# A transformer block on one core: the first MLP matrix by Strassen's scheme on 2x2 blocks

## Chip, core and metric

One core of a Trainium2 chip runs the whole block in one launch. The metric is the device time of a launch in microseconds (us). Engines are called PE or TensorE (matrix products), DVE or VectorE, ACT or ScalarE, POOL or GpSimd, and SP, which issues DMA transfers. PEld is the load of a matmul's stationary tile. Every engine works through its own list of instructions in order; an instruction waits for the results and the free buffers that it needs.

## What is computed

One layer on T = 1024 tokens of width D = 1024, in float32: RMS norm, a wide input projection, two kinds of attention (A: dilated windows; B: compressed, selected and windowed blocks, with gates), an output projection added to the residual, RMS norm, an MLP of width 4096 with squared ReLU, and a last RMS norm:

```
h_res = h_res + mixed @ w_out
h = rms_norm(h_res, norm_mlp)
h_res = h_res + square(relu(h @ w_up)) @ w_down
return rms_norm(h_res, norm_final)
```

## The kernel before

Each float32 product is made of three matmuls: a tile is split into hi (rounded) and lo (the rest), and hi x hi, hi x lo, lo x hi are summed in PSUM. `split` makes both: a copy on ACT, a subtraction on DVE (L94 and L95, or L97 and L98 with a scale); where the source is a product, POOL subtracts (L1035).

Up to about 690 us the kernel makes projections and attention. The list `ORD = [5, 7, 6, 4, 3, 2, 1, 0]` is the order of the eight 128-token tiles in attention B. The output projection is cut into pieces (`out_proj(i, half)`, half 0 for A's heads, half 1 for B's) that are pumped into the attention as its tiles get ready; a piece makes 12 matmuls for 512 columns into a bank F (L704 to L706), and DVE adds it to the residual rows `hr(i)` (tiles called `st`, L708). The last pieces, of tiles 1 and 0, follow the attention. Before each, POOL sums a tile's heads into `ob` (L842), PE transposes `ob`, ACT and DVE split it (`mh`, `ml`) and L704 begins.

In the MLP, tokens 512 to 1023 (`H0`) come first. `h2_step` transposes rows of `hr`, scales by the gain and splits into `h2h`, `h2l`; rows are not normalised there, the factor 1/(mean square + eps) is applied when down is added (L1061, `r2q`). w_up is cut into 32 feature tiles f of 128 columns. `up(f)` makes for each token half 8 x 3 matmuls of 512 columns (L1024 to L1026), and `up_act` the squared ReLU: ACT relu, DVE product (L1033), ACT copy `uh` (L1034), POOL `ul` (L1035). `down(f0, t, last)` takes two feature tiles, one 128-token tile and two column cuts: 6 matmuls each (L1058 to L1060), which DVE adds to `hr(t)` (L1061). The main loop makes up for the next two feature tiles while down uses the two of before; weights arrive as 512 KB blocks (`wur`, `wdr`) one or two tiles ahead, in buffers of their own. PSUM has four banks in turn for `up` and `dn`. No order is written out by hand here: the scheduler of the framework sets it from dependencies, priorities and buffers.

## Time and profile before

| | us |
|---|---|
| median of 3 runs | 1425.83 (1423.37 to 1430.28) |
| the profiled execution's own time | 1424.83 |
| span in its profile (first to last instruction) | 1423.0 |
| TensorE busy | 1350.6 |
| VectorE, ScalarE, GpSimd busy | 791.9, 621.3, 478.7 |

The span is one execution's. "Busy" sums the time in which an engine runs an instruction; a busy TensorE is not one at its peak. An idle engine that nobody waits for costs nothing. The granted clock is that of TensorE, 1.00 for the upper of its two levels.

### The profile page before, as it was taken

The page shows a single profiled execution, that of the slowest core. Times are in us where ns is not written, and L with a number is a line of the kernel's source. Part 1 is how long each engine was busy: PE and PEld are TensorE (multiplying, and loading weights), DVE is VectorE, ACT ScalarE, POOL GpSimd, SP SyncE. Part 2 cuts the span into 40 slices and gives each one's busy share as a digit, 9 for nine tenths or more (in the row PEclk, how much of TensorE's full clock was granted, in tenths as well). Part 3 has the DMA queues.
Part 4 walks back from the last instruction along what each step waited for, and adds up shares of the span by engine and source line. Part 5 has one row for each costly group of instructions (what it writes and reads, how often), then busy time and mean ns, then how long its engine had stood idle before and what let it go on. Part 6 is the DMA issues. An engine that isn't in the chain of part 4 may idle for free.

```text
span 1423.0 us, 23380 instructions
## 1 busy us (share of the span) xinstructions
PE 1350.6 (95%) x9083; PEld 1144.6 (80%) x9083; DVE 791.9 (56%) x1624; ACT 621.3 (44%) x1108; POOL 478.7 (34%) x704
## 2 busy tenths in 40 slices
...
PEclk9999999999999999999899999999999999999999
...
GB/s 187 67 123 123 89 166 63 208 186 129 88 152 180 167 146 132 149 130 107 118 104 45 30 47 58 60 45 30 56 49 60 45 30 59 45 60 45 1 0 118
DMA packets 285198, 131.64 MB, mean 93 GB/s; under 512 B 219040, under 2 KB 272288, under 8 KB 285088
## 3 DMA queue, kind: packets, MB, share of 16 engines
...
## 4 chain that ended last, share of the span: by engine, by line
PE 71%; DVE 8%; DMA 7%; issue 5%; POOL 4%; ACT 4%; SPq 1%; POOLq 0%; DVEq 0%; ACTq 0%
PE dn L1060 8%; PE dn L1058 8%; PE dn L1059 8%; PE up L1026 8%; PE up L1025 8%; PE up L1024 8%; PE F L334 3%; PE F L335 3%; PE F L336 3%; DMA pt<-hl 2%; PE T L359 2%; PE S L417 2%; PE S L419 1%; DVE ns L428 1%; ACT ns L433 1%
## 5 line engine op out<-in xcount | busy, mean ns | idle before, releaser
L1035 POOL TENSOR_TENSOR ul<-ua,uh 128x512 fp32r<-128x512 f32 x64 | 83.6, 1306 | 608.2 <-ACT uh L1034 608.2
L1061 DVE SCALAR_TENSOR_TENSOR st<-dn,r2q,st 128x512 f32<-128x512 f32 (+1 forms) x257 | 191.8, 747 | 157.6 <-PE dn L1060 157.6
L1060 PE MATMUL dn<-wdh,ul 128*128 128x512 f32 (+1 forms) x514 | 202.6, 394 | 0.0
L1058 PE MATMUL dn<-wdh,uh 128*128 128x512 f32 (+1 forms) x514 | 202.4, 394 | 0.0
L1059 PE MATMUL dn<-wdl,uh 128*128 128x512 f32 (+1 forms) x514 | 202.3, 394 | 0.0
L1024 PE MATMUL up<-h2h,wuh 128*128 128x512 f32 x480 | 187.1, 390 | 1.0 <-ACT wuh L94 1.0
L1026 PE MATMUL up<-h2h,wul 128*128 128x512 f32 x480 | 187.0, 390 | 0.5 <-DVE wul L95 0.5
L1025 PE MATMUL up<-h2l,wuh 128*128 128x512 f32 x480 | 187.0, 390 | 0.0
L334 PE MATMUL F<-wh,hh 128*128 128x256 f32 (+1 forms) x576 | 166.3, 290 | 6.7 <-DVE st L213 3.2
L335 PE MATMUL F<-wl,hh 128*128 128x256 f32 (+1 forms) x576 | 165.6, 288 | 2.4 <-DVE wl L95 2.4
L336 PE MATMUL F<-wh,hl 128*128 128x256 f32 (+1 forms) x576 | 164.6, 286 | 0.0
L1032 ACT ACTIVATE ua<-up 128x512 f32<-128x512 f32 x60 | 35.5, 591 | 230.9 <-PE up L1026 230.9
L433 ACT ACTIVATE ns<-ns,mn 128x640 f32<-128x640 f32 (+7 forms) x152 | 110.8, 748 | 35.1 <-POOL mn L432 20.8
L449 POOL TENSOR_TENSOR hl<-ns,hl 128x640 f16<-128x640 f32 (+5 forms) x67 | 105.6, 1577 | 33.2 <-ACT hl L447 26.9
L334 PEld LDWEIGHTS F<-wh,hh 128*128 128x128 f32 x576 | 109.6, 191 | 8.9 <-DVE st L213 3.6
L1059 PEld LDWEIGHTS dn<-wdl,uh 128*128 128x128 f32 x514 | 96.5, 188 | 23.1
L1060 PEld LDWEIGHTS dn<-wdh,ul 128*128 128x128 f32 x514 | 96.4, 188 | 23.1
L1058 PEld LDWEIGHTS dn<-wdh,uh 128*128 128x128 f32 x514 | 96.5, 188 | 22.5
L95 DVE TENSOR_TENSOR wul<-wur,wuh 128x1024 fp32r<-128x1024 f32 x32 | 39.5, 1234 | 134.7 <-ACT wuh L94 134.7
L335 PEld LDWEIGHTS F<-wl,hh 128*128 128x128 f32 x576 | 110.4, 192 | 3.8 <-DVE wl L95 3.2
L336 PEld LDWEIGHTS F<-wh,hl 128*128 128x128 f32 x576 | 110.1, 191 | 0.5
L1024 PEld LDWEIGHTS up<-h2h,wuh 128*128 128x128 f32 x480 | 90.1, 188 | 20.8 <-ACT wuh L94 1.4
...
## 6 DMA issues: line engine op xcount, KB each, us to landing
wur<-in_w_up_dram SPq DMA_DIRECT2D x32, 512.0 KB, 4.1
wdr<-in_w_down_dram SPq DMA_DIRECT2D x32, 512.0 KB, 4.2
wr<-in_w_in_dram SPq DMA_DIRECT2D x44, 256.0 KB, 2.9
st<-in_x_dram SPq DMA_DIRECT2D x8, 512.0 KB, 6.0
wor<-in_w_out_dram SPq DMA_DIRECT2D x16, 256.0 KB, 3.6
ns<-in_xT_dram SPq DMA_DIRECT2D x7, 512.0 KB, 5.4
out_dram<-st SPq DMA_DIRECT2D x7, 512.0 KB, 2.6
w<-in_w_k_dram SPq DMA_DIRECT2D x4, 512.0 KB, 5.5
```

Source lines behind the costliest of these rows:

```text
L334: pe.matmul(ps, hh[:, k, ts], hi, start=k == 0, stop=False)
L335: pe.matmul(ps, hh[:, k, ts], lo, start=False, stop=False)
L336: pe.matmul(ps, hl[:, k, ts], hi, start=False, stop=k == KD - 1)
L433: u["exp"] = act.activation(ns[:, :n * 128], ns[:, :n * 128], AF.Exp, scale=-1.0, bias=mn[:, j:j + 1])
L449: pool.tensor_sub(lo, p, hi)
L1024: pe.matmul(ps, hi[:, k], h2h[:, k, hs], start=k == 0, stop=False)
L1025: pe.matmul(ps, hi[:, k], h2l[:, k, hs], start=False, stop=False)
L1026: pe.matmul(ps, lo[:, k], h2h[:, k, hs], start=False, stop=k == KD - 1)
L1058: pe.matmul(ps, uh[:, ts], wh[:, cs], start=j == 0, stop=False)
L1059: pe.matmul(ps, uh[:, ts], wl[:, cs], start=False, stop=False)
L1060: pe.matmul(ps, ul[:, ts], wh[:, cs], start=False, stop=j == NB - 1)
L1061: dve.scalar_tensor_tensor(o[:, cs], ps, r2q[:, t:t + 1], o[:, cs], op0=OP.mult, op1=OP.add)
```

## The change

Both factors of the first MLP product are cut into 2x2 blocks: w_up for a pair g of feature tiles into four blocks of 512 x 128 (k halves and the two tiles), the tokens into halves H0 and H1. Seven block products of 4 x 3 matmuls replace eight; there are 16 rounds g. The stationary tiles are sums of w_up's blocks, made per round (`w_prep`: five named combinations, then `w_split` into `wa` to `we`); the moving ones are sums of token blocks B11, B21, B22, T1 to T4, made once (`h2_first` for H0, `h2_second` for H1, which needs both halves). Sums of products, in float32, are made on DVE out of PSUM (`up`), and `c_done` makes the squared ReLU, `uh` and `ul`. For the sums to hold, rows must be normalised before they are combined: `out_proj`'s half 1 now squares, takes a power (L722 in the changed kernel) and scales `hr(i)` in place.

Memory is laid out anew: tiles of 128 x 512 float32 (2 KB in a partition) share places by `tag`. `u2` and `u3` hold quarters of w_down as they land (`d_load`) and later `uh` and `ul` of the second feature tile for H1; `cA` and `cB` hold two w_up blocks and later `c12` and `c22`. All PSUM tiles of the MLP come from the banks T, O, F (two each or fewer) and S (three) of the attention stage; down uses S.

```diff
@@ -706,6 +711,17 @@
                 pe.matmul(ps, ml[:, k], wh[:, cs], start=False, stop=k == 3)
             o = hr(i)[:, cs]
             dve.scalar_tensor_tensor(o, ps, rmm[:, half, i:i + 1], o, op0=OP.mult, op1=OP.add)
+            if half == 0:
+                return
+            if c == 0:
+                st["q"] = wop.tile([128, T], BF, name="mhq", tag="mh", bufs=2)
+            act.activation(st["q"][:, cs], o, AF.Square, accum_out=ssq[:, i, c:c + 1])
+            if c == 1:
+                r = r2[:, i:i + 1]
+                dve.tensor_scalar(r, ssq[:, i, 0:1], ssq[:, i, 1:2], D * EPS, op0=OP.add, op1=OP.add)
+                pool.tensor_tensor(r, r, expo[:, :1], op=OP.pow)
+                for n in range(2):
+                    mv(n, hr(i)[:, n * 512:n * 512 + 512], hr(i)[:, n * 512:n * 512 + 512], i, r2)
 
         return [prep] + [lambda c=c: part(c) for c in range(T // WC)]
...
+    def w_prep(g, first=False):
+        if g >= NP:
+            return []
+        A11, A12, A21, A22 = (RW[g, b] for b in range(4))
+
+        def s1():
+            if not first:
+                w_split(g, 1, "a", A11)
+            w_split(g, 4, "d" if first else "b", A22)
+
+        def s2():
+            dve.tensor_sub(A11, A11, A21)
+            dve.tensor_add(A21, A21, A22)
+            dve.tensor_sub(A22, A22, A11)
+            w_split(g, 6, "c", A22)
+
+        def s3():
+            if not first:
+                w_split(g, 2, "d", A12)
+            dve.tensor_sub(A12, A12, A22)
+
+        def s4():
+            w_split(g, 7, "e", A11)
+
+        return [s1, s2, s3, s4]
...
+    def d_load(g, q):
+        j, c = q % 2, q // 2
+        t = RD[g, q] = small("u%d" % (2 + j))
+        sp.dma_start(t, A["w_down"][(2 * g + j) * 128:(2 * g + j + 1) * 128, c * 512:c * 512 + 512])
+
+    def d_split(g, q):
+        j, c = q % 2, q // 2
+        if c == 0:
+            WD[g, j] = ml[0].tile([128, 2, D], F32R, name="dn", bufs=2)
+        t = WD[g, j][:, :, c * 512:c * 512 + 512]
+        split(t[:, 0], t[:, 1], RD.pop((g, q)))
...
+    UT = {(0, 0): ("v0", "v1"), (1, 0): ("v2", "v3"), (0, 1): ("u0", "u1"), (1, 1): ("u2", "u3")}
+
+    def c_done(g, f, h, a):
+        hi, lo = U[g, f, h] = [small(x, F32R, "uh" if n == 0 else "ul") for n, x in enumerate(UT[f, h])]
+        dve.scalar_tensor_tensor(a, a, 0.0, a, op0=OP.max, op1=OP.mult)
+        act.activation(hi, a, AF.Copy)
+        pool.tensor_sub(lo, a, f32(hi))
+
+    def up(g):
+        y = {n: bank(x, [128, 512], 2) for n, x in ((1, "T"), (4, "O"), (6, "T"), (2, "F"), (7, "O"), (5, "S"), (3, "S"))}
+        for q in range(2):
+            d_load(g, q)
+        prod(g, 1, y[1])
+        c11 = small("u0", name="c11")
+        act.activation(c11, y[1], AF.Copy)
+        w_split(g, 5, "a", RW[g, 2])
+        for q in range(2):
+            d_split(g, q)
+        for q in range(2, 4):
+            d_load(g, q)
+        prod(g, 4, y[4])
+        prod(g, 6, y[6])
+        c12 = small("cA", name="c12")
+        dve.tensor_add(c12, y[6], c11)
+        w_split(g, 3, "b", RW[g, 1])
+        w_load(g + 1, 2, "r2")
+        w_load(g + 1, 1, "r3")
+        prod(g, 2, y[2])
+        dve.tensor_add(c11, y[2], c11)
+        c_done(g, 0, 0, c11)
+        prod(g, 7, y[7])
+        c22 = small("cB", name="c22")
+        dve.tensor_add(c22, y[7], c12)
+        c21 = small("u1", name="c21")
+        dve.scalar_tensor_tensor(c21, y[4], -1.0, c22, op0=OP.mult, op1=OP.add)
+        c_done(g, 1, 0, c21)
+        for q in range(2, 4):
+            d_split(g, q)
+        prod(g, 5, y[5])
+        dve.tensor_add(c22, y[5], c22)
+        dve.tensor_add(c12, y[5], c12)
+        c_done(g, 1, 1, c22)
+        prod(g, 3, y[3])
+        dve.tensor_add(c12, y[3], c12)
+        c_done(g, 0, 1, c12)
...
+            ps = bank("S", [128, 512])[:, :cs.stop - cs.start]
+            for j in range(2):
+                uh, ul = U[g, j, h]
+                wd = WD[g, j]
+                pe.matmul(ps, uh[:, ts], wd[:, 0, cs], start=j == 0, stop=False)
+                pe.matmul(ps, uh[:, ts], wd[:, 1, cs], start=False, stop=False)
+                pe.matmul(ps, ul[:, ts], wd[:, 0, cs], start=False, stop=j == 1)
+            dve.scalar_tensor_tensor(o[:, cs], ps, r2[:, t:t + 1], o[:, cs], op0=OP.mult, op1=OP.add)
...
+    def h2_second(j):
+        raw = ml[0].tile([128, 4, 512], F32, name="wdx", tag="dn", bufs=2)
+        T1, T2, T3, T4 = (raw[:, n] for n in range(4))
+        ps = h2_ps(H1, j)
+        g = gm32[:, j:j + 1]
+        act.activation(T3, ps, AF.Copy, scale=g)
+        dve.scalar_tensor_tensor(T1, ps, g, f32(XH["B11"][:, j]), op0=OP.mult, op1=OP.subtract)
+        dve.tensor_sub(T1, T1, f32(XL["B11"][:, j]))
+        ps = h2_ps(H1, j + 4)
+        g = gm32[:, j + 4:j + 5]
+        dve.scalar_tensor_tensor(T2, ps, g, T1, op0=OP.mult, op1=OP.subtract)
+        dve.scalar_tensor_tensor(T3, ps, g, T3, op0=OP.mult, op1=OP.subtract)
+        split(XH["B22"][:, j], XL["B22"][:, j], ps, scale=g)
+        pool.tensor_sub(T4, T2, f32(XH["B21"][:, j]))
+        dve.tensor_sub(T4, T4, f32(XL["B21"][:, j]))
+        for x, t, e in (("T2", T2, dve), ("T3", T3, pool), ("T4", T4, dve), ("T1", T1, pool)):
+            act.activation(XH[x][:, j], t, AF.Copy)
+            e.tensor_sub(XL[x][:, j], t, f32(XH[x][:, j]))
...
+    for g in range(NP):
+        last = g == NP - 1
+        if g:
+            up(g)
...
+            fin["j"] = ml[0].tile([128, D], F32, name="sqj", tag="we", bufs=1)
+        else:
+            w_load(g + 1, 0, "cA")
+            w_load(g + 1, 3, "cB")
+        jobs = [] if last else w_prep(g + 1)
+        for i, t in enumerate(TO):
+            down(g, t, last)
+            if i >= 2 and jobs:
+                jobs.pop(0)()
```

**Order on POOL at the end of the attention stage.** `ot`, `oc`, `ob` are the head sums of a tile, `rmm` the norm factor of half 1, `ul` the rest of an activation. Before:

```order
L842 TENSOR_TENSOR oc_9790<-ot0_9937,oc_9790 128x512
L840 TENSOR_TENSOR den_10327<-den_10327,gate_81 128x8
L841 TENSOR_TENSOR ot_10142<-ot_10142,den_10327 128x8x64
L842 TENSOR_TENSOR ob_10141<-ot_10142,oc_9790 128x512
L117 TENSOR_TENSOR rmm_560<-ssm_559,expo_59 128x1
L1035 TENSOR_TENSOR ul_10362<-ua_10487,uh_10361 128x512
```

Now, where `r2` is the power of a row's sum of squares (the first one is tile 1's, the second tile 0's):

```order
L857 TENSOR_TENSOR ot_10191<-ot_10191,den_10383 128x8x64
L722 TENSOR_TENSOR r2_563<-r2_563,expo_59 128x1
L858 TENSOR_TENSOR ob_10190<-ot_10191,oc_9827 128x512
L117 TENSOR_TENSOR rmm_567<-ssm_566,expo_59 128x1
L722 TENSOR_TENSOR r2_563<-r2_563,expo_59 128x1
L1073 TENSOR_TENSOR ul_10774<-c11_10594,uh_10773 128x512
L1171 TENSOR_TENSOR T1l_10415<-wdx_10601,T1h_10408 128x512
L1167 TENSOR_TENSOR wdx_10601<-wdx_10601,B21h_10406 128x512
L1171 TENSOR_TENSOR T3l_10417<-wdx_10601,T3h_10410 128x512
L1171 TENSOR_TENSOR T1l_10415<-wdx_10629,T1h_10408 128x512
```

Behind tile 1's last piece a power now stands between the two steps that make tile 0's `ob`, and twelve subtractions for T1, T4 and T3 follow, where only the `ul` rows stood.

**Order on DVE where the second token half is made.** Before, each step is one split out of a transposed bank T (`h2l`), then weight splits:

```order
L98 SCALAR_TENSOR_TENSOR h2l_10349<-T_10590,gvec_58,h2h_10348 128x512
L98 SCALAR_TENSOR_TENSOR h2l_10349<-T_10603,gvec_58,h2h_10348 128x512
L95 TENSOR_TENSOR wdl_10656<-wdr_10648,wdh_10655 128x1024
L95 TENSOR_TENSOR wdl_10665<-wdr_10648,wdh_10664 128x1024
L95 TENSOR_TENSOR wul_10661<-wur_10649,wuh_10660 128x1024
L1033 SCALAR_TENSOR_TENSOR ua_10628<-O_10522,ua_10628 128x512
L95 TENSOR_TENSOR wul_10670<-wur_10652,wuh_10669 128x1024
L1033 SCALAR_TENSOR_TENSOR ua_10633<-F_10523,ua_10633 128x512
```

Now, in one step j (`wdx` holds T1 to T4 in float32; B11l, B22l, T2l, T4l are lo parts):

```order
L1164 SCALAR_TENSOR_TENSOR wdx_10629<-T_10638,gm32_564,wdx_10629 128x512
L1165 SCALAR_TENSOR_TENSOR wdx_10629<-T_10638,gm32_564,wdx_10629 128x512
L1171 TENSOR_TENSOR T4l_10418<-wdx_10601,T4h_10411 128x512
L1171 TENSOR_TENSOR T2l_10416<-wdx_10629,T2h_10409 128x512
L98 SCALAR_TENSOR_TENSOR B22l_10414<-T_10638,gm32_564,B22h_10407 128x512
L1168 TENSOR_TENSOR wdx_10629<-wdx_10629,B21l_10413 128x512
L1160 SCALAR_TENSOR_TENSOR wdx_10672<-T_10673,gm32_564,B11h_10405 128x512
L1161 TENSOR_TENSOR wdx_10672<-wdx_10672,B11l_10412 128x512
L1171 TENSOR_TENSOR T4l_10418<-wdx_10629,T4h_10411 128x512
L1164 SCALAR_TENSOR_TENSOR wdx_10672<-T_10681,gm32_564,wdx_10672 128x512
L1165 SCALAR_TENSOR_TENSOR wdx_10672<-T_10681,gm32_564,wdx_10672 128x512
L1171 TENSOR_TENSOR T2l_10416<-wdx_10672,T2h_10409 128x512
```

Where one row per bank stood, some nine stand for two banks, half of them with both inputs in SBUF.

**Order on DVE and PE in a round of the MLP.** Before, on DVE (`ua` is the squared ReLU, `st` the residual, x7 means seven rows alike):

```order
L1033 SCALAR_TENSOR_TENSOR ua<-up,ua 128x512
L1061 SCALAR_TENSOR_TENSOR st<-dn,r2q,st 128x512 x7
L1033 SCALAR_TENSOR_TENSOR ua<-up,ua 128x512
L95 TENSOR_TENSOR wul<-wur,wuh 128x1024
L1061 SCALAR_TENSOR_TENSOR st<-dn,r2q,st 128x512
L1033 SCALAR_TENSOR_TENSOR ua<-up,ua 128x512
L1061 SCALAR_TENSOR_TENSOR st<-dn,r2q,st 128x512 x7
L95 TENSOR_TENSOR wdl<-wdr,wdh 128x1024 x2
```

Now (rows of one round; `dn` is a quarter of w_down, c11 to c22 the four blocks of the result):

```order
L95 TENSOR_TENSOR dn_13111<-u2_13090,dn_13111 128x512
L1101 SCALAR_TENSOR_TENSOR c21_13186<-O_13084,c22_13184 128x512
L95 TENSOR_TENSOR dn_13114<-u3_13092,dn_13114 128x512
L1071 SCALAR_TENSOR_TENSOR c21_13186<-c21_13186 128x512
L1106 TENSOR_TENSOR c22_13184<-S_13088,c22_13184 128x512
L1107 TENSOR_TENSOR c12_13145<-S_13088,c12_13145 128x512
L1071 SCALAR_TENSOR_TENSOR c22_13184<-c22_13184 128x512
L1110 TENSOR_TENSOR c12_13145<-S_13089,c12_13145 128x512
L95 TENSOR_TENSOR dn_13111<-u2_13117,dn_13111 128x512
L95 TENSOR_TENSOR dn_13114<-u3_13119,dn_13114 128x512
L1071 SCALAR_TENSOR_TENSOR c12_13145<-c12_13145 128x512
L1127 SCALAR_TENSOR_TENSOR st_5707<-S_13238,r2_563,st_5707 128x512
```

Between the last products and the first evacuation of down stand sums, squares and the splits of w_down; L1110 reads product 3's bank behind the square of `c22`.

On PE, before, down's chunks (`dn`) and up's matmuls alternate with weights split a round ahead:

```order
L1058 MATMUL dn_11611<-wdh_11441,uh_11379 128x512
L1059 MATMUL dn_11611<-wdl_11442,uh_11379 128x512
L1060 MATMUL dn_11611<-wdh_11441,ul_11380 128x512
L1024 MATMUL up_11655<-h2h_10348,wuh_11446 128x512
L1025 MATMUL up_11655<-h2l_10349,wuh_11446 128x512
L1026 MATMUL up_11655<-h2h_10348,wul_11447 128x512
L1024 MATMUL up_11655<-h2h_10348,wuh_11446 128x512
L1025 MATMUL up_11655<-h2l_10349,wuh_11446 128x512
```

Now (F is product 2 of the next round, S the chunks of down):

```order
L1064 MATMUL F_13388<-B21l_10413,wd_13330 128x512
L1065 MATMUL F_13388<-B21h_10406,wd_13330 128x512
L1063 MATMUL F_13388<-B21h_10406,wd_13330 128x512
L1064 MATMUL F_13388<-B21l_10413,wd_13330 128x512
L1124 MATMUL S_13238<-dn_13111,uh_13167 128x512
L1125 MATMUL S_13238<-dn_13111,uh_13167 128x512
L1065 MATMUL F_13388<-B21h_10406,wd_13330 128x512
L1126 MATMUL S_13238<-dn_13111,ul_13168 128x512
L1124 MATMUL S_13238<-dn_13114,uh_13188 128x512
L1125 MATMUL S_13238<-dn_13114,uh_13188 128x512
```

Six chunks of down follow there, all of tokens H0, and then product 4 of the next round with the weight tile `wb`, which is split out of `cB`.

## Rows read from the trace of the kernel before

**Rows 1.** The page: the span, TensorE's busy time with its share and instructions, and the clock granted in 40 equal slices (tenths).
```profile
span 1423.0 us, 23380 instructions
PE 1350.6 (95%) x9083; PEld 1144.6 (80%) x9083; DVE 791.9 (56%) x1624; ACT 621.3 (44%) x1108; POOL 478.7 (34%) x704
PEclk9999999999999999999899999999999999999999
```

**Rows 2.** Busy time of each engine (us, instructions) in two stretches; behind it the granted clock, the mean busy share of the DMA engines, GB/s.
```profile
600.00:620.00 20.00, 18.34 (x215) 14.83 (x213) 17.54 (x43) 16.72 (x32) 13.48 (x16) 1.00 0.85 156
760.00:1400.00 640.00, 640.00 (x2781) 521.77 (x2780) 276.73 (x356) 128.29 (x179) 77.40 (x62) 1.00 0.14 42
```

**Rows 3.** Waits from 760 to 1400 us: VectorE's for TensorE, total us, times, longest.
```profile
DVE st L1061 <- PE dn L1060: 154.0, 180, 2.5
```

**Rows 4.** Timeline of PE in the MLP: start, us of one, engine, line, operation, tiles.
```profile
1001.01 0.39 PE L1024 MATMUL up<-h2h,wuh 128*128 128x512 f32 x1
1003.73 0.39 PE L1024 MATMUL up<-h2h,wuh 128*128 128x512 f32 x1
...
1004.41 0.40 PE L1058 MATMUL dn<-wdh,uh 128*128 128x512 f32 x1
1009.77 0.39 PE L1060 MATMUL dn<-wdh,ul 128*128 128x512 f32 x1
```

**Rows 5.** Groups of instructions from 760 to 1400 us: shapes, count, busy us, mean ns; idle before and what ended it.
```profile
L1061 DVE SCALAR_TENSOR_TENSOR st<-dn,r2q,st 128x512 f32<-128x512 f32 x238 | 178.5, 750 | 154.1 <-PE dn L1060 154.0
L1035 POOL TENSOR_TENSOR ul<-ua,uh 128x512 fp32r<-128x512 f32 x57 | 73.8, 1294 | 550.3 <-ACT uh L1034 550.3
L1033 DVE SCALAR_TENSOR_TENSOR ua<-up,ua 128x512 f32<-128x512 f32 x57 | 39.2, 688 | 78.7 <-ACT ua L1032 78.7
L1034 ACT ACTIVATE uh<-ua 128x512 fp32r<-128x512 f32 x57 | 36.0, 632 | 78.5 <-DVE ua L1033 78.5
```

**Rows 6.** The same from 0 to 700 us: the power on GpSimd.
```profile
L117 POOL TENSOR_TENSOR rmm<-ssm,expo 128x1 f32<-128x1 f32 x16 | 9.0, 565 | 11.7 <-DVE ssm L116 11.3
```

**Rows 7.** Timeline at the end of the attention stage, all engines: `ob` of tile 0, tile 1's last matmul, the transposes, the addition, a Square with its accumulator, a power.
```profile
689.10 1.19 POOL L842 TENSOR_TENSOR ob<-ot,oc 128x512 f32<-128x512 f32 x1
689.92 0.39 PE L706 MATMUL F<-woh,ml 128*128 128x512 f32 x1
690.32 0.63 ACT L850 ACTIVATE ot<-ob 128x512 f32<-128x512 f32 x1 [3.44 <-POOL ob L842]
690.35 0.66 PE L359 MATMUL T<-c_ident,ob 128*128 128x128 f32 x4
690.35 0.75 DVE L708 SCALAR_TENSOR_TENSOR st<-F,rmm,st 128x512 f32<-128x512 f32 x1 [2.73 <-PE F L706]
690.86 0.19 ACT L850 ACTIVATION_READ_ACCUMULATOR ot<-ob 128x1 f32 x1
691.31 0.55 POOL L117 TENSOR_TENSOR rmm<-ssm,expo 128x1 f32<-128x1 f32 x1 [1.02 <-DVE ssm L116]
```

**Rows 8.** Timeline: tile 0's last addition on DVE; the last up matmul of the first two feature tiles and the first of the next.
```profile
700.92 0.75 DVE L708 SCALAR_TENSOR_TENSOR st<-F,rmm,st 128x512 f32<-128x512 f32 x1 [1.80 <-PE F L706]
726.10 0.39 PE L1026 MATMUL F<-h2h,wul 128*128 128x512 f32 x1
727.49 0.50 PE L1024 MATMUL up<-h2h,wuh 128*128 128x512 f32 x1 [0.99 <-ACT wuh L94]
```

**Rows 9.** Timeline of VectorE and GpSimd at three places: 17 to 27 us, 714 us, 732 to 734 us.
```profile
17.90 2.88 DVE L95 TENSOR_TENSOR w0l<-wr,w0h 128x512 fp32r<-128x512 f32 x1
17.23 5.82 POOL L281 TENSOR_TENSOR acc<-acc,ns 128x1024 f32<-128x1024 f32 x2 [1.14 <-ACT ns L280]
26.52 0.69 DVE L95 TENSOR_TENSOR w0l<-wr,w0h 128x512 fp32r<-128x512 f32 x1
...
714.17 2.54 POOL L1035 TENSOR_TENSOR ul<-ua,uh 128x512 fp32r<-128x512 f32 x2 [22.31 <-ACT uh L1034]
714.71 0.75 DVE L98 SCALAR_TENSOR_TENSOR h2l<-T,gvec,h2h 128x512 fp32r<-128x512 f32 x1 [0.22 <-ACT h2h L97]
...
731.37 1.23 DVE L95 TENSOR_TENSOR wdl<-wdr,wdh 128x1024 fp32r<-128x1024 f32 x1 [0.34 <-ACT wdh L94]
731.94 1.82 POOL L1035 TENSOR_TENSOR ul<-ua,uh 128x512 fp32r<-128x512 f32 x1 [15.22 <-ACT uh L1034]
732.84 2.00 DVE L95 TENSOR_TENSOR wdl<-wdr,wdh 128x1024 fp32r<-128x1024 f32 x1 [0.24 <-ACT wdh L94]
```

**Rows 10.** Matmuls of 512 columns before and after the clock came back, and the window's row (columns as in rows 2).
```profile
682.43 0.63 PE L704 MATMUL F<-woh,mh 128*128 128x512 f32 x1
687.86 0.40 PE L706 MATMUL F<-woh,ml 128*128 128x512 f32 x1
680.00:700.00 20.00, 18.73 (x90) 13.96 (x88) 9.02 (x14) 6.60 (x13) 5.36 (x8) 0.85 0.38 95
```

**Rows 11.** The page's DMA issues (count, KB each, median us to landing), and one issue of w_in on SP with the ACT copy that waited for it.
```profile
wr<-in_w_in_dram SPq DMA_DIRECT2D x44, 256.0 KB, 2.9
wur<-in_w_up_dram SPq DMA_DIRECT2D x32, 512.0 KB, 4.1
338.66 0.38 SPq L183 DMA_DIRECT2D wr<-in_w_in_dram  x1
341.43 0.63 ACT L94 ACTIVATE wh<-wr 128x512 fp32r<-128x512 f32 x1 [2.30 <-DMA wr<-in_w_in_dram]
```

More of the change, by code (lines that the diff above doesn't have):

```diff
@@ L1037, in up_half @@
[L1037 to L1050 removed]
+    e2 = cst.tile([128, NT], F32, name="e2")
+    H0 = 1 - ORD[-1] // 4
+    H1 = 1 - H0
+    TO = [h * 4 + t for h in (H0, H1) for t in range(4)]
```

262 lines of the change are left out of this document (112 added, 150 removed).

## Prediction

> **What bounds the kernel now.** I read the page's totals first: TensorE is busy for 95% of the span [rows 1]. The table by stage shows that this is two programs. From 760 us on, the MLP rounds keep TensorE busy for all of 640 us at full clock, with VectorE at 43%, ScalarE at 20% and GpSimd at 12% [rows 2]; the waits there say the same, since VectorE's 154 us of idle time all end with a matmul [rows 3]. In that stretch time is the number of matmuls times their spacing. Before 700 us the engines are balanced: in 600 to 620 PE, VectorE and ScalarE are busy 18.3, 17.5 and 16.7 us of 20 [rows 2], so work added to any of them lengthens something. Between the two lies the transition, about 690 to 730 us.
>
> **The gain.** From 1001.01 to 1003.73 us twelve up matmuls start, 0.2267 us apart; from 1004.41 to 1009.77 there are 23 spacings of down matmuls, 0.233 us each [rows 4]. The change makes 84 matmuls of 96 for a pair of feature tiles. Round 0 belongs to the transition (below); 15 rounds of 12 fewer give 180 x 0.2267 = -40.8 us, if TensorE stays the bound. Down is unchanged. All else is on the other side of the ledger.
>
> **Added in the attention stage.** Each of eight output tiles gets two Squares on ScalarE (0.63, and 0.19 to read the accumulator [rows 7]) and half of an in-place scaling (0.63 by L1034 [rows 5]): 2.27 us; on VectorE a small operation and the other half (0.69 at most, by L1033), on GpSimd one power (0.565) [rows 6]. Tiles 1 and 0 are in the terms below; six tiles make 13.6 us of ScalarE. Hidden entirely it is 0, since ScalarE idles 3.3 us of 20; entirely on the path it is 13.6. It goes into gaps, but PE, VectorE and ScalarE take turns as the bound there, so I take about a third: **+4**. The Squares that go from 725 to 740 stood beside other work and give nothing back.
>
> **Hand-over.** In before the last matmul of tile 1 starts at 689.92 while GpSimd makes `ob` (689.10 to 690.29); PE goes on at 690.35 with the transposes of `ob` [rows 7]. In the changed order tile 1's power (L722) stands ahead of `ob` on GpSimd, in order. It needs both Squares, so: F ends 690.3, VectorE adds it by 691.1 (0.75), Square and accumulator 691.9 (0.82), the small sum 692.1, power 692.7 (0.55), `ob` 693.9 (1.19). PE's next row needs `ob`, and nothing else stands ahead of it: **+3.6** (3.3 to 4.5).
>
> **Transition.** In before the first two feature tiles are done when the last up matmul has streamed, 726.10 + 0.23 = 726.3 [rows 8]; VectorE had 8 splits of 0.75 to make there. In the changed order the second token half goes through `h2_second`. Its start: tile 0's last row of F is added from 700.92 [rows 8]; 8 up matmuls that PE made ahead of it are gone (-1.84), the hand-over adds 3.6, so the add ends at 703.4. VectorE then has 15 rows before the first `T1`: four PSUM splits (3.0), eight of 0.69 (5.5: weight splits and combinations, one scaling, `c11`) and three small ones (0.45), so `T1` starts at 712.4. From it to the last `T4l` are 38 rows: 18 that read PSUM (0.66 spacing, 11.9 us) and 20 with both inputs in SBUF (0.61, 12.2 us), by the 0.69 to 0.75 that one lasts, less overlap. That is 24 us. But GpSimd has 13 subtractions of the same size there, at 1.27 (a little under L1035's mean [rows 5]) 16.5 us, and the two do not run together: at 17.90 VectorE's `w0l`, 0.69 alone, takes 2.88 beside GpSimd's `acc`; `wdl` takes 2.00 from 732.84 while `ul` runs, and `ul` itself 1.82 behind the `wdl` before it. A VectorE row that reads PSUM is not held (0.75 at 714.71 beside `ul`) [rows 9]. So the port is taken for 12.2 + 16.5 = 28.7 us; with the PSUM rows never beside GpSimd it is 40.6. The PSUM rows of one j are independent of the GpSimd rows of the one before, so most overlap: 31. Last `T4l` 743.4, last product 743.9, against 726.3; of that difference of 17.6, 3.6 is the hand-over. In before 1.0 us of PE idle follows [rows 8]; after, `c21`, its square, `uh` and `ul` follow (0.7 + 0.7 + 0.6 + 1.3), of which down's first chunks cover half: 0.7 more. **+14.7** (11 to 25). PE has only 60 matmuls and 32 transposes there, some 18 us.
> The Trainium skill ("SBUF — State Buffer", section "SBUF: two separate sides") says that the port pair of VectorE and GpSimd is a lock held for a whole instruction, which a VectorE instruction with two SBUF inputs must take too; the rows above agree. By it the stretch takes 28.7 us at least; were the port no lock it would be 24, and the sum 7 us lower.
>
> **Clock.** After a gap of PE the 512-column matmuls last 0.63 us instead of 0.39 and the granted clock is 0.85 in 680 to 700 [rows 10]: the lower of the two levels, for some us. The two new gaps can bring it back; PE waits there anyway: **+2** (0 to 5).
>
> **Each round.** PE has 84 x 0.2267 + 96 x 0.233 = 41.4 us. VectorE: 16 evacuations (0.75), 4 squares, 7 sums, 11 splits and 4 combinations (0.69), 30 us; ScalarE 16 rows of 0.63, 10 us; GpSimd 4 of 1.3. None is the bound; two chains may be. (a) `u2` and `u3` hold a quarter of w_down, then the next quarter, then `uh` and `ul`. The first loads can start only after the last down matmul of the round before (z). Then: load, split (0.63 + 0.69), load, split, `uh` 0.63, `ul` 1.3, load into cB, split 0.63, product 4 of the next round. PE reaches product 4 after products 7's end, 5, 3 and 2 (37 x 0.2267) and six down chunks (36 x 0.233), at z + 16.8. A load of 256 KB takes 2.9, one of 512 KB (here a pair of 256) 4.1; SP's issue at 338.66 lets ScalarE start at 341.43, 2.77 later [rows 11]. With 2.9 for each the chain is 13.9 us, with 4.1 17.5: from 2.9 of slack to 0.7 late, before anything queues. (b) Product 3's bank is freed by the sum at L1110, which stands behind the square of `c22` on VectorE, and that behind GpSimd's `ul` by the port: up to 1.3, and one of three banks is missing for down's first chunks. Stall of a round 0 to 1.4, nearer the lower end since PE's 16.8 covers 2.9-us loads: 0.6 x 15 = **+9**.
> The end is alike: the same rows follow the last matmul, only a column replaces EPS: 0.
>
> **Sum.** -40.8 + 4 + 3.6 + 14.7 + 2 + 9 = -7.5. The profiled run took 1424.83, 1.0 under the median of 1425.83; against the median, 1418.3: **1418 us**.
>
> **Rivals.** (B) Rounds are covered. PE's 16.8 us hide chain (a), the bank costs nothing, and the transition is at the lock's 28.7: -9 - 2.3 more gives 1407. For it: 2.9-us loads, DMA engines 14% busy in the rounds [rows 2]. Against: the port and VectorE's order between. Chance 0.27. (C) **Slower**: chain (a) bounds every round. If each of its three loads takes 4.1 (two at once, as `wur`) and the queue and port on the way cost 1.5, the round is 17.5 + 1.5 - 16.8 = 2.2 us late: 33 instead of 9, 1442. It decides from a loss of 1.1 us per round on (16.5 us of net gain over 15 rounds). For it: each round has one such chain and nothing prefetches w_down any more. Against: in before loads land in 2.9. Chance 0.23. (D) Products run at down's spacing of 0.233, since both change the weights and the moving tile with each matmul: 84 x 15 x 0.0063 = +8, no change, 1426. Up of before did so too at 0.2267. Chance 0.10. My forecast, 0.40, has its own range 1410 to 1426.
>
> **Numbers.** A measurement of this kernel tells 0.5%, 7.1 us, from no change: faster is under 1418.7. Of the forecast half lies under it (0.20, with B 0.47), the rest is no change, with most of D 0.28; C is the slower 0.25 with the forecast's edge. The range 1402 to 1437 leaves out B's lower tail (no attention cost, no clock loss) and the half of C above break-even plus 1.3 us a round.
>
> **What would show it.** Up to 590 us both traces should agree. GpSimd's row `ob` should start about 3 us later behind L722. The last L1171 should end near 743 with VectorE's L1171 and L1168 rows lengthened to 1.2 to 2 us beside GpSimd's. In the rounds 41.4 + 0.6 us between equal rows; the idle time of PE should stand before L1063 of product 4 (waiting for `wb`) or before L1124 (VectorE's L1110 or `st`). I am wrong if PE has no idle time after 760 (then B), if the gaps are before loads of over 3.5 us (C), or if products start 0.233 apart (D).

## Result and the profile after

The changed kernel takes **1414.72 us** (median of 5 runs, 1410.85 to 1416.60), the one before 1424.91 beside it: ratio **0.9919 [0.9894, 0.9944]**. The forecast was 1418. The profiled execution took 1414.72 us, its span is 10.1 us shorter than before's.

The page after, against [rows 1]: span, TensorE's busy time, the granted clock in 40 slices.

```profile
span 1412.9 us, 23742 instructions
...
PE 1313.4 (93%) x8891; PEld 1110.6 (79%) x8891; DVE 970.4 (69%) x1953; ACT 650.3 (46%) x1212; POOL 512.0 (36%) x724
...
PEclk9999999999898999999999999999999999999998
```

TensorE lost 37 us of busy time and the span only 10: idle time came in. The end of the attention stage with the transition in before, then the same stretch and the rounds in after (columns as in [rows 2]):

```profile
690.00:760.00 70.00, 68.19 (x328) 55.08 (x327) 36.96 (x47) 36.57 (x58) 10.65 (x9) 1.00 0.29 91
...
690.00:760.00 70.00, 52.31 (x241) 37.55 (x241) 57.56 (x83) 36.07 (x66) 28.59 (x23) 0.93 0.14 41
760.00:1400.00 640.00, 632.45 (x2755) 515.44 (x2754) 448.11 (x654) 156.84 (x266) 97.47 (x70) 1.00 0.17 53
```

In the rounds TensorE is no longer busy all the time; VectorE went from 43% to 70%. The transition has 18 us without a matmul. What PE waited for in the rounds, and VectorE's wait that answers to [rows 3]: total us, times, longest.

```profile
DVE st L1127 <- PE S L1126: 69.7, 58, 3.1
...
PE S L1124 <- DVE c L1110: 5.9, 14, 0.6
```

VectorE's wait for down's chunks was more than halved, and PE now waits for VectorE about once in each round: at L1110, the sum that frees product 3's bank. The place in one round, from the timeline of PE:

```profile
1006.86 0.39 PE L1126 MATMUL S<-dn,ul 128*128 128x512 f32 x1
1007.61 0.50 PE L1124 MATMUL S<-dn,uh 128*128 128x512 f32 x1 [0.37 <-DVE c L1110]
1007.95 0.39 PE L1125 MATMUL S<-dn,uh 128*128 128x512 f32 x1
```

Two spacings of 0.75 and 0.34 us stand where two of 0.227 would: 0.64 us lost. The next such row of L1124 starts at 1049.20, so a round takes 41.59 us. The chain of waits of that next round tells what comes last there (start, us, what):

```profile
1038.56 3.02 DMA u<-in_w_down_dram
...
1041.66 0.64 ACT dn L94
...
1042.33 0.52 DVE dn L95
...
1042.94 0.69 DVE c L1101
1043.62 0.62 DVE dn L95
1044.24 1.71 DVE c L1071
1045.95 0.60 DVE c L1106
1046.55 0.60 DVE c L1107
...
1048.47 0.69 DVE c L1110
...
1049.20 0.50 PE S L1124
```

A load of w_down (started when the place `u2` came free), its split, and then VectorE's queue in order: the split holds up the sums, and the square L1071 takes 1.71 us instead of 0.69 while GpSimd's `ul` runs from 1044.12. In the groups of the page `ul` (L1073) has a mean of 1454 ns, against 1294 in [rows 5]; VectorE's square (L1071) has 1151 from 760 to 1400 us.

The matmuls themselves, timeline of PE (product 2 of a round, then chunks of down), against [rows 4]:

```profile
1002.78 0.39 PE L1063 MATMUL F<-B21h,wd 128*128 128x512 f32 x1
...
1004.14 0.39 PE L1063 MATMUL F<-B21h,wd 128*128 128x512 f32 x1
...
1010.24 0.39 PE L1124 MATMUL S<-dn,uh 128*128 128x512 f32 x1
...
1014.09 0.39 PE L1126 MATMUL S<-dn,ul 128*128 128x512 f32 x1
```

Six spacings of a product are 1.36 us, 0.2267 each. The 17 spacings of down are 3.85 us: 0.2265 each, where before had 0.233. Nothing in the prediction lets down become faster. Over all rows of down the mean spacing is 0.2330 us before and 0.2272 after (waits left out), which makes 8.9 us for the 1530 matmuls. DMA issues of after (count, KB, us to landing; [rows 11]):

```profile
u<-in_w_down_dram SPq DMA_DIRECT2D x64, 256.0 KB, 2.8
...
r<-in_w_up_dram SPq DMA_DIRECT2D x32, 256.0 KB, 2.7
```

w_up is also stored in another order for the changed kernel, outside the launch: each of its 512 x 128 blocks lies in one piece of 256 KB. The section on the change does not say so, and no run shows what it gives or would cost inside the launch.

Hand-over in after, against [rows 7]: timeline of VectorE, GpSimd and some rows of PE.

```profile
690.19 0.75 DVE L713 SCALAR_TENSOR_TENSOR st<-F,rmm,st 128x512 f32<-128x512 f32 x1 [3.30 <-PE F L711]
...
690.99 0.50 PE L709 MATMUL F<-woh,mh 128*128 128x512 f32 x1
...
693.89 0.20 PE L468 MATMUL O<-v,ptx 128*128 128x65 f16 x1
...
694.09 0.75 DVE L713 SCALAR_TENSOR_TENSOR st<-F,rmm,st 128x512 f32<-128x512 f32 x1 [3.15 <-PE F L711]
...
694.75 0.22 DVE L854 TENSOR_SCALAR den<-ot,vsc 128x8 f32<-128x8 f32 x1
...
695.29 0.21 POOL L856 TENSOR_TENSOR den<-den,gate 128x8 f32<-128x8 f32 x1 [4.42 <-DVE den L855]
...
696.58 0.55 POOL L722 TENSOR_TENSOR r<-r,expo 128x1 f32<-128x1 f32 x1
...
697.10 1.19 POOL L858 TENSOR_TENSOR ob<-ot,oc 128x512 f32<-128x512 f32 x1
```

`ob` starts 3.0 us after tile 1's last addition; in before it started 1.25 us ahead of it [rows 7]. The power L722 stands ahead of it, as foretold, but costs it only some 0.5 us: the step before, `ot` (L857), ends at 696.62. More comes from PE: tile 1's second piece (twelve matmuls from 690.99) is now ahead of the attention's last products (L468, 693.89), so VectorE's `den` and GpSimd's `den` come behind the addition, not before it. PE's transposes of `ob` start at 698.33, 4.24 us behind the start of that addition; in before both start at 690.35 [rows 7].

Transition in after, against [rows 8] and [rows 9]: timeline of the first row of `h2_second`, two rows beside each other at the port, the last `T4l`, the last product, and PE behind it.

```profile
708.43 0.75 DVE L713 SCALAR_TENSOR_TENSOR st<-F,rmm,st 128x512 f32<-128x512 f32 x1 [1.47 <-PE F L711]
...
718.30 0.74 DVE L1160 SCALAR_TENSOR_TENSOR wdx<-T,gm,B11h 128x512 f32<-128x512 f32 x1
...
743.28 1.74 POOL L1167 TENSOR_TENSOR wdx<-wdx,B21h 128x512 f32<-128x512 f32 x1
...
743.80 1.77 DVE L1171 TENSOR_TENSOR T2l<-wdx,T2h 128x512 fp32r<-128x512 f32 x1
...
748.98 0.67 DVE L1171 TENSOR_TENSOR T4l<-wdx,T4h 128x512 fp32r<-128x512 f32 x1
...
750.13 0.39 PE L1065 MATMUL S<-T4h,wd 128*128 128x512 f32 x1
...
751.75 0.50 PE L1124 MATMUL S<-dn,uh 128*128 128x512 f32 x1 [1.23 <-DVE c L1214]
...
754.21 0.63 PE L1125 MATMUL S<-dn,uh 128*128 128x512 f32 x1
```

From 718.30 to 749.65 are 31.35 us. The last product streams until 750.36, 24.0 later than before's 726.33; a matmul of 0.63 at 754.21 shows the lower level of the clock (granted 0.57 in 753 to 757 us).

### The profile page after: what moved, and what is told of

Its sections match the earlier page's. It is cut to its first block, busy times and chain, and to the rows that moved or that the text cites. A ratio compares the mean times of both kernels' runs of the same rounds, so it can differ in the third digit from the quotient of the medians.

```text
span 1412.9 us, 23742 instructions
## 1 busy us (share of the span) xinstructions
PE 1313.4 (93%) x8891; PEld 1110.6 (79%) x8891; DVE 970.4 (69%) x1953; ACT 650.3 (46%) x1212; POOL 512.0 (36%) x724
## 4 chain that ended last, share of the span: by engine, by line
PE 57%; DVE 16%; DMA 8%; issue 7%; POOL 6%; ACT 5%; SPq 1%; DVEq 0%; POOLq 0%; ACTq 0%
PE S L1124 8%; PE S L1125 7%; PE S L1126 7%; PE F L335 3%; PE F L336 3%; PE F L337 3%; DMA u<-in_w_down_dram 3%; PE O L1064 2%; PE O L1063 2%; PE T L1065 2%; PE T L1063 2%; PE T L1064 2%; PE O L1065 2%; PE S L418 2%; DVE c L1071 1%
## 5 line engine op out<-in xcount | busy, mean ns | idle before, releaser
L1073 POOL TENSOR_TENSOR ul<-c,uh 128x512 fp32r<-128x512 f32 x64 | 92.5, 1454 | 557.8 <-ACT uh L1072 555.9
L1127 DVE SCALAR_TENSOR_TENSOR st<-S,r,st 128x512 f32<-128x512 f32 (+1 forms) x257 | 185.8, 742 | 70.3 <-PE S L1126 69.7
L1124 PE MATMUL S<-dn,uh 128*128 128x512 f32 (+1 forms) x514 | 203.2, 396 | 9.6 <-DVE c L1110 5.9
L1126 PE MATMUL S<-dn,ul 128*128 128x512 f32 (+1 forms) x514 | 200.6, 391 | 0.8 <-POOL ul L1073 0.8
L1125 PE MATMUL S<-dn,uh 128*128 128x512 f32 (+1 forms) x514 | 200.8, 391 | 0.0
L1124 PEld LDWEIGHTS S<-dn,uh 128*128 128x128 f32 x514 | 97.2, 189 | 37.8 <-DVE c L1110 12.2
L1126 PEld LDWEIGHTS S<-dn,ul 128*128 128x128 f32 x514 | 97.0, 189 | 22.0 <-POOL ul L1073 1.5
L1125 PEld LDWEIGHTS S<-dn,uh 128*128 128x128 f32 x514 | 97.4, 190 | 19.2
L448 ACT ACTIVATE hl<-ns 128x640 f16<-128x640 f32 (+5 forms) x115 | 91.2, 802 | 5.8 <-DMA pt<-hl 5.0
L468 PE MATMUL O<-v,pt 128*128 128x65 f16 x694 | 77.3, 195 | 15.9 <-DMA pt<-hl 13.4
L468 PEld LDWEIGHTS <-pt 128*128 128x128 f16 x694 | 63.9, 99 | 27.6 <-DMA pt<-hl 17.4
L418 PE MATMUL S<-kb,qb 128*128 128x384 f32 (+3 forms) x192 | 72.9, 385 | 12.6 <-DVE mn L429 8.9
```

What stands on the lines that cost most here:

```text
L418: pe.matmul(ps[:, :w], u["q"], u["k"][:, cs], start=True, stop=False)
L468: pe.matmul(ps, ph, v[:, 64:129], start=t == 0, stop=False)
L1073: pool.tensor_sub(lo, a, f32(hi))
L1124: pe.matmul(ps, uh[:, ts], wd[:, 0, cs], start=j == 0, stop=False)
L1125: pe.matmul(ps, uh[:, ts], wd[:, 1, cs], start=False, stop=False)
L1126: pe.matmul(ps, ul[:, ts], wd[:, 0, cs], start=False, stop=j == 1)
```

## Experiments

Ratios are against the kernel before on the same chip. The theories: down's new pace comes from where its weights lie (the layout) and not from the scheme; the wait of each round is VectorE's lateness, started by the load of w_down, and not a lack of banks; the 31 us of the transition are the port that VectorE and GpSimd share.

**1. The layout without the scheme.** The kernel before, with 128 empty bytes ahead of the MLP's pool. By the layout of the built programs down's weights start 96 bytes past a multiple of 256 in before, 224 past one after the change; here 224.

```diff
+    mlq.tile([128, 32], F32, name="pad")
```

> The kernel before with one empty tile of 128 bytes per partition ahead of the MLP's left-hand tiles: the split down weights start at 224 instead of 96 bytes past a multiple of 256; no instruction changes. Theory A (the changed kernel's down matmuls start 0.2267 us apart, those of before 0.233, because of where the down weights lie in memory): down's spacing falls to 0.227 and the time by 1536 x 0.006 = 9 us, to about 1416. Theory B (the spacing comes from the changed kernel's rounds, its banks or its order): spacing stays 0.233 and the time 1425.

Measured 1415.60 us (6 runs, 1413.61 to 1421.05), ratio **0.9906 [0.9881, 0.9931]**: all of the change's gain, with no product removed. Chunks of down, timeline of PE:

```profile
1006.96 0.39 PE L1058 MATMUL dn<-wdh,uh 128*128 128x512 f32 x1
...
1011.72 0.39 PE L1058 MATMUL dn<-wdh,uh 128*128 128x512 f32 x1
```

21 spacings in 4.76 us, 0.2267 each, against 0.233 in [rows 4]. From tile 1's last addition to the end this run takes 722.4 us and before 732.7, 10.3 less; after takes 718.9.

**2. The scheme without the layout.** The changed kernel, with the tile that holds down's weights (and shares its place with `wdx`) moved by 128 bytes, to 96 past a multiple of 256.

```diff
-            WD[g, j] = ml[0].tile([128, 2, D], F32R, name="dn", bufs=2)
+            WD[g, j] = ml[0].tile([128, 2112], F32R, name="dn", bufs=2)[:, 32:2080].rearrange("p (a b) -> p a b", a=2)
```

> The changed kernel with its down weights (and T1 to T4 in float32, which share the place) moved by 128 bytes, to 96 past a multiple of 256; every other address keeps its remainder. Theory A: down's spacing rises from 0.227 to 0.233, the time by 9 us to about 1424, and nothing is left of the gain. Theory B: 0.227 and 1415 as before the move.

Measured 1422.68 (12 runs, 1419.54 to 1428.50), ratio **0.9967 [0.995, 0.9984]**. Down is back at before's pace, 17 spacings in 3.96 us, 0.233:

```profile
1020.27 0.40 PE L1124 MATMUL S<-dn,uh 128*128 128x512 f32 x1
...
1024.23 0.39 PE L1126 MATMUL S<-dn,ul 128*128 128x512 f32 x1
```

So the scheme by itself is worth 0.0033 x 1427.56 = 4.7 us (2.3 to 7.1), and the place of one tile some 7 of the change's 10 to 12 (by medians and by the ratio). The rest of the new layout is still in these 4.7: the output projection's weights start at 96 in before and at 224 in both versions of the changed kernel, and what that gives was not run by itself.

**3. Which places are quick.** Two versions of the kernel before, run once each: all of down's weights at a multiple of 256 (40 empty columns in place of 32), and the eight weight tiles at eight places, 32 bytes apart.

```diff
+    mlq.tile([128, 40], F32, name="pad")
```

> The kernel before with a pad of 160 bytes: all down weights start exactly on a multiple of 256 bytes by the program's addresses. If only the distance to a multiple of 256 counts and the nearer the better, down's spacing is 0.227 as with the 128-byte pad; if the good place is the one where the other fast tiles lie (224 past it), it stays at 0.231 or more.

```diff
-            hi = mlq.tile([128, D], F32R, name="wdh", bufs=NB + 2)
-            lo = mlq.tile([128, D], F32R, name="wdl", bufs=NB + 2)
+            hi, lo = (mlq.tile([128, D + 8], F32R, name="%s%d" % (x, f % 4), bufs=1)[:, :D] for x in ("wdh", "wdl"))
```

> The kernel before with eight separate tiles for the split down weights, each 32 bytes longer, so that the hi and lo tiles of four feature tiles start 96, 128, 160, 192, 224, 0, 32 and 64 bytes past a multiple of 256. Theory A: the spacing behind L1057, L1058, L1059 differs from tile to tile, 0.233 at 96 and 0.227 at 224; the others tell the rule. Theory B: 0.233 for all.

At a multiple of 256: 1427.43 us, no gain. Timeline of PE: 21 spacings in 4.91 us, 0.234.

```profile
1005.91 0.40 PE L1058 MATMUL dn<-wdh,uh 128*128 128x512 f32 x1
...
1010.82 0.40 PE L1058 MATMUL dn<-wdh,uh 128*128 128x512 f32 x1
```

The eight places: 1428.32 us, no gain; a single run of each says little, the spacings more. They do not go by the tile. In the rounds that use the tile at 224, it is left after 0.2268 us in the first matmul of a chunk and after 0.2327 in the third; in the other rounds the tile at 96 is left after 0.232 and 0.228. All others lie between 0.230 and 0.236, with no order by distance. Nor is 0.233 one spacing in before: with all eight tiles at 96, spacings of 0.237 and 0.229 alternate there. So neither theory came out. What can be said is that weights all at 224 are quick, and all at 0 or all at 96 slow; why was not found. The stationary tiles `uh` and `ul` start at 224 in before, in after and in all versions of experiments 1 to 4 (layout of the built programs), so a rule on the distance between the two tiles cannot be told from one on the moving tile's own place: no run moves the stationary ones.

**4. Is it so elsewhere too?** Experiment 1, with the weights and inputs of the input projection also at 224 (256-column matmuls); in short:

```diff
+    htp.tile([128, 32], F32, name="padh")
+    wp.tile([128, 32], F32, name="padw")
-            hi = wp.tile([128, k, w], F32R, name="wh", bufs=5)
-            lo = wp.tile([128, k, w], F32R, name="wl", bufs=5)
+            hi, lo = (wp.tile([128, 576], F32R, name=x, bufs=5)[:, :k * w].rearrange("p (k w) -> p k w", k=k)
+                      for x in ("wh", "wl"))
+    w0p.tile([128, 48], F32, name="padx")
+    mlq.tile([128, 32], F32, name="pad")
```

> The kernel before with the pad of 128 bytes and, in the first stage, the split projection weights and the normalised inputs moved to 224 past a multiple of 256 as well (their five places had five different remainders). If the spacing hangs on the place there too, the projection's 256-column matmuls fall from 0.123 us towards 0.114 and, where TensorE is the bound there, 5 to 10 us come off b_pad128: 1406 to 1411 where the kernel before takes 1426. If other engines bound that stage, the time stays at b_pad128's, ratio 0.99.

1418.55 us (1414.60 to 1421.77), ratio 0.9918 [0.9901, 0.9936], no better than experiment 1. The projection's weights had lain at 32, 96, 160 and 224 in before. The median of its spacings is 0.120 us, 0.118 in before (means, with those up to 0.3 us, 0.125 and 0.1235): there the place gains nothing.

**5. Banks or VectorE?** The changed kernel with product 3 in a bank T, so that all three banks S are down's.

```diff
-... (7, "O"), (5, "S"), (3, "S"))}
+... (7, "O"), (5, "S"), (3, "T"))}
```

> The changed kernel with product 3 in a bank T instead of S. Theory C (PE's wait of 0.3 to 0.6 us at the first down chunk of each round comes from the bank that product 3 holds until the sum at L1110): those waits go, 14 x 0.64 = 9 us with their slow first matmuls, to 1406. Theory D (it comes from the late rows of VectorE, behind the w_down load, and any bank will do): another wait takes its place, on uh or ul, and under 3 us are gained.

1416.24 (1412.17 to 1418.62), ratio 0.9908 [0.9886, 0.993]: no change. PE's wait from 760 to 1400 us:

```profile
PE S L1124 <- DVE st L1127: 4.7, 13, 0.4
```

The same wait under another name: now it is the evacuation behind L1110 that is late. VectorE is, not the banks.

**6. What makes VectorE late.** The first two quarters of w_down land in `v2` and `v3` (free earlier) instead of `u2` and `u3`.

```diff
-        t = RD[g, q] = small("u%d" % (2 + j))
+        t = RD[g, q] = small(("v%d" if c == 0 else "u%d") % (2 + j))
```

> The changed kernel with w_down's first two quarters landing in v2 and v3 (free when the down chunks of tokens 512 to 1023 are done, about 11 us before the round's end) instead of u2 and u3. Theory D (VectorE is late at L1110 and L1127 because its splits of w_down wait for a load that can start only at the round's end): VectorE's rows come about 3 us earlier, the waits of PE at the first chunks go, 13 x 0.6 and part of the last round's 4: 8 to 10 us less, about 1406 where the kernel before takes 1426. Theory C2 (VectorE is late because of its own work and the port it shares with GpSimd): the waits stay, 1414 to 1416.

1412.09 (1408.60 to 1413.59), ratio 0.9894 [0.9869, 0.9919]; span 1406.8, 6.1 shorter. The wait of the same rows:

```profile
PE S L1124 <- DVE c L1110: 0.3, 2, 0.2
```

PE's wait of each round is all but gone, 5.9 to 0.3 us. The chain that starts with w_down's load was its cause. The gain foretold, 8 to 10 us, did not come whole. In the rounds the starts of PE's matmuls show 6.5 us less above 0.2267 each (11.2 in after, 4.7 here), but from tile 1's last addition to the end the run is only 4.1 shorter (714.7 against 718.9), since the transition became longer; the other 2.0 of the span lie ahead, where the edit changes nothing. Between the medians are 2.6 us with overlapping intervals, so the times alone do not show a gain.

**7. The normalisation in the attention stage.** No Squares, no powers, no scaling in place: `out_proj` returns after the addition and `r2` is a constant, so the output is another.

```diff
+    dve.memset(r2, 0.03125)
...
-            if half == 0:
-                return
+            return
```

> The changed kernel without the Squares, powers and in-place scaling of the output projection's second half; the rows go on unnormalised, so the output is another. If these cost what the two traces show between them (3.7 us up to tile 1's last addition, 4.3 at the hand-over, 1.4 up to tile 0's last addition), tile 0's last addition comes at 699 instead of 708 and the time is 9 us less, about 1406. If the delay comes from elsewhere (other addresses, another order) it stays.

1408.93 (1403.94 to 1411.08), ratio 0.9865 [0.9828, 0.9902], 5.8 us under the changed kernel by the medians and not the 9 expected, at the edge of what the intervals tell. The hand-over has before's order again, `ob` 1.25 us ahead of tile 1's last addition (696.14). Timeline:

```profile
692.94 0.22 DVE L854 TENSOR_SCALAR den<-ot,vsc 128x8 f32<-128x8 f32 x1
...
694.89 1.19 POOL L858 TENSOR_TENSOR ob<-ot,oc 128x512 f32<-128x512 f32 x1
```

From tile 1's last addition to tile 0's last are 9.2 us here, 14.3 in after, 10.6 in before: the norm of the last two tiles costs some 5 us there (14.2 to 15.0 in all seven kernels that have it, 10.5 to 10.6 in the five with before's code). But tile 1's last addition comes at 696.14, later than in after (694.09), which has the work of the norm. Over all kernels run, it starts at 690.35 to 696.93 without that work and at 689.46 to 694.30 with it (experiments 2, 5, 6, 8 and after; later, 695.22 and 694.83, where experiments 9 and 10 hold the piece back). The spread is there before any of that work: the first matmul of the output projection starts at 415.38 in before, 420.48 in after, 420.47 in experiment 1, whose code up to there is before's. From it to tile 1's last addition are 275.0 us in before, 273.6 in after. So the six tiles ahead cost nothing that can be seen.

**8. The shared port.** GpSimd's twelve subtractions of `h2_second` go to VectorE.

```diff
-        pool.tensor_sub(T4, T2, f32(XH["B21"][:, j]))
+        dve.tensor_sub(T4, T2, f32(XH["B21"][:, j]))
...
-        for x, t, e in (("T2", T2, dve), ("T3", T3, pool), ("T4", T4, dve), ("T1", T1, pool)):
+        for x, t, e in (("T2", T2, dve), ("T3", T3, dve), ("T4", T4, dve), ("T1", T1, dve)):
```

> The changed kernel with GpSimd's 12 subtractions of h2_second on VectorE. Theory L (VectorE and GpSimd hold one port in turn, so GpSimd's share takes nothing off VectorE): 24 + 12 x 0.61 = 31.3 us from the first T1 to the last T4l, as now (31.35), time unchanged within 2 us. Theory P (they run side by side): 7 us more.

1418.16 (1410.79 to 1420.10), ratio 0.993 [0.9899, 0.9961], not told apart from the changed kernel. VectorE's timeline: 713.80 to 744.06 is 30.3 us, 1.1 less than in after, with 48 rows on VectorE instead of 38 (the twelve are in, and two that stood ahead of the last `T4l` in after, a split of w_down and a sum, come behind it). With these two at 0.60 each it would be 31.5, the 31.35 of after.

```profile
713.80 0.74 DVE L1160 SCALAR_TENSOR_TENSOR wdx<-T,gm,B11h 128x512 f32<-128x512 f32 x1
...
739.71 0.68 DVE L1171 TENSOR_TENSOR T2l<-wdx,T2h 128x512 fp32r<-128x512 f32 x1
...
743.38 0.68 DVE L1171 TENSOR_TENSOR T4l<-wdx,T4h 128x512 fp32r<-128x512 f32 x1
```

Were the two able to work side by side, twelve rows of 0.61 more would have cost about 7 us. As it is they took turns: of VectorE's twelve rows L1168 and L1171 in after, four last 1.72 to 1.77, two 1.10 and 1.11 and six 0.67 to 0.83, while here the rows L1168 and L1171 take 0.67 to 0.69. The Trainium skill ("SBUF — State Buffer", section "SBUF: two separate sides") says that a VectorE instruction with two inputs in SBUF and a GpSimd instruction that reads SBUF hold the shared port pair in turn, as a lock; these traces agree, with 1.77 us for `T2l` at 743.80 in after and 0.68 at 739.71 here.

**9. The order of the hand-over.** Experiment 6, and tile 1's second piece held back until the attention's last products are issued.

```diff
+            last_pv[:] = [pe.matmul(ps, pl, v[:, 64:129], start=False, stop=t == n - 1)]
...
+            if (half, i, n) == (1, ORD[-2], 2):
+                credit[0] = min(credit[0], 1)
+                return
...
+        with tc.issue_after(last_pv[0].ins) if n == 0 else ExitStack():
+            pieces.pop(0)[3]()
```

> The changed kernel with w_down landing in v2 and v3 (a_land_v) and tile 1's second piece of the output projection held behind the last value matmul of the attention, which puts the order of before back there: VectorE makes tile 0's den between tile 1's two additions, GpSimd makes ob ahead of tile 1's power. If that order is what made the hand-over long (14.4 us from tile 1's second addition to tile 0's second, 10.5 in before), the stretch falls to about 11 and the time by 3 us against a_land_v, to 1409 where the kernel before takes 1426. If the added Squares and power make it long, it stays 14 and the time 1412.

**1407.93** (1407.10 to 1408.29), ratio **0.9846 [0.9833, 0.986]**. The order came as meant: `den` 692.70 and `ob` 694.66 stand ahead of tile 1's last addition at 695.22. But the time was not won there. Timeline:

```profile
694.66 1.18 POOL L859 TENSOR_TENSOR ob<-ot,oc 128x512 f32<-128x512 f32 x1
...
698.99 1.09 PE L360 MATMUL T<-c_ident,ob 128*128 128x128 f32 x4 [3.81 <-DVE B11l L98]
```

PE transposes `ob` 3.15 us after it is done, since the bank waits for VectorE's `B11l`; from tile 1's last addition to tile 0's last are 14.5 us, as in after. `B11l` needs ScalarE's `B11h`, and ScalarE, in order, stood idle for tile 1's last addition, because its Square comes first:

```profile
696.00 0.63 ACT L719 ACTIVATE mhq<-st 128x512 bf16<-128x512 f32 x1 [3.34 <-DVE st L714]
...
697.37 1.27 ACT L97 ACTIVATE B11h<-T,gm 128x512 fp32r<-128x512 f32 x2
```

So the order of before alone does not shorten the stretch; with experiment 7 (9.2 us without the norm) this says that the work of the norm makes it long, as the expectation's second theory has it: here through its place in ScalarE's queue. The profiled executions of this kernel and of experiment 6 lie 0.65 us apart (1407.95, 1408.60), their medians, of different chips, 4.2. That the time is under both of the expected ones, and what the held piece itself gives, stays open.

**10. All together.** Experiment 9 with the first-stage weights and inputs placed as in experiment 4:

```diff
+    wp.tile([128, 32], F32, name="padw")
...
+            hi, lo = (wp.tile([128, 576], F32R, name=x, bufs=5)[:, :k * w].rearrange("p (k w) -> p k w", k=k)
+                      for x in ("wh", "wl"))
...
+    w0p.tile([128, 56], F32, name="padx")
```

> a_hold with the first stage's tiles moved as in b_align. If both gains hold they add up: 5 to 10 us under a_hold, 1400 to 1405; Strassen's products then still give 5 us over b_align. If the first stage is not bound by TensorE, it is a_hold again.

**1405.43** (1403.31 to 1407.96), ratio **0.9831 [0.9815, 0.9847]**: quicker than both kernels, and not told apart from experiment 9.

## Why the prediction came out as it did

The time came out 3.6 us under the forecast, inside its own range. That the number is so near is luck: its sum, -7.5, matches the spans' -10.1 only because a term that it did not have made up for terms that were too small. Term by term (profiled executions; each measured number from the starts of rows in the two traces):

| term | predicted | measured |
|---|---|---|
| 12 matmuls fewer in 15 rounds | -40.8 | -40.8 |
| down's spacing | 0 | -8.9 |
| attention stage, to tile 1's last addition | +4 | +3.7, no cost of the change |
| from there to the last product of round 0 | +17.6 | +20.3 |
| behind it, with the clock | +0.7 + 2 | +2.1 |
| rounds | +9 | +10.1 |
| last round | 0 | +4.7 |
| sum | -7.5 | -8.8 (spans: -10.1) |

Of the 1.3 us between the sum and the spans, 0.7 are three matmuls of down that PE makes ahead of round 0's last product; the rest is in means that differ in the fourth place.

**The products.** Right: 0.2267 a matmul, 84 of them a round. Rival D (products at 0.233) is out.

**Down.** "Down is unchanged" is the step that failed. The diff said that the memory was laid out anew, and the prediction took that for a matter of which places are shared; the start of a tile had no price. Experiments 1 and 2 show it from both sides: the layout without the scheme gives 0.9906, the scheme without the layout 0.9967. Had down kept its pace, the time would have been the 1422.68 of experiment 2, which on its own chip is 4.9 us under before: 2.6 short of the -7.5, which lies just outside the 2.3 to 7.1 of experiment 2. The sign of the remaining sum was right. From tile 1's last addition to the end, experiment 2 takes 728.9 us, 3.8 less than before.

**Attention stage.** The +4 has no support. The +3.7 of these two traces lies inside the spread of the same point in kernels with and without the work, and the traces were 5.1 apart before the first piece of that work (experiment 7); that both should agree up to 590 us was wrong for the same reason. Hidden entirely, which the prediction gave as its lower end, is what the traces bear out.

**Hand-over and transition.** Tile 1's last to tile 0's last addition: 10.57 us before, 14.34 after, +3.8; predicted was +3.6 for `ob` less 1.84 for the up matmuls that went, so 2.0 too little. Experiment 7 parts the two: the norm costs 5.1, and without it the stretch is 1.4 shorter than before's. The mechanism was right in part. The power does stand ahead of `ob`, but delays it by 0.5; the rest is that PE, whose order the prediction had not looked at, made the second piece ahead of the attention's last products, so `den` came late, and that after the gap PE runs at the lower level (granted 0.66 in 698 to 703 us), which the prediction priced under the clock. Then 9.1 us from the end of that addition to `T1` (predicted 9.0), 31.35 from `T1` to the last `T4l` (31), 0.7 to the end of the products (0.5). The port's lock priced this well. Rows that were to lengthen to between 1.2 and 2 us did so in part: six of twelve, four of them to over 1.7 (experiment 8).

**Clock and what follows.** The granted clock of 690 to 760 us fell from 1.00 to 0.93, and PE's waits at 751.75 and 753.61 are for VectorE's sums and `uh`. Behind the last product these make +2.1 against +2.7; what the clock costs ahead of it is in the +20.3.

**Rounds.** 0.6 us predicted; at the place foretold 0.41 to 0.89 in each of 14 rounds, 9.2 in all (0.64 at 1007.61; 41.59 us from there to 1049.20 for 180 matmuls), and 0.9 more at product 4 in four of them. The prediction gave chain (a), the loads, and chain (b), product 3's bank, as two possible causes. It is one chain through both: the load of w_down delays VectorE's queue, the queue delays L1110. Experiment 5 takes the bank away and the wait stays; experiment 6 takes the load's late start away and it goes. Rival C needed loads of 4.1 us; they take 2.8. Rival B needed no idle time of PE after 760 us; there is some in nearly each round.

**The last round.** Costed at nothing ("the same rows follow the last matmul"). In every other round product 2 of the next one covers VectorE's sums; in the last there is no next one. Between 1377 and 1385 us PE waits four times for `uh`, `ul` and L1110, 0.27 to 0.71 us each; with the slow spacings around them that is 4.7 us, 1.4 of them at the lower level of the clock behind the last wait (granted 0.54 in 1382 to 1385).
